# Log-sum-exp of 16384 rows: other groups of rows for each exponential and row sum

## The chip, the cores and the metric

The kernel runs on one core of a Trainium2 chip. The metric is the device time of one execution in microseconds, taken as the median of several runs. Besides that there is one profiled execution with its trace. The engines that matter here are ScalarE (ACT in the profile), VectorE (DVE), TensorE (PE), SyncE (SP), which issues the transfers, and the 16 DMA engines, which carry them.

## The reference

x has the shape 32 x 512 x 1024 in float32, 67 MB in all. For each of the 16384 rows of 1024 elements the log of the sum of the exponentials is wanted:

```python
max_x = np.max(x, axis=-1, keepdims=True)
return (max_x.squeeze(-1) + np.log(np.sum(np.exp(x - max_x), axis=-1))).astype(np.float32)
```

## The kernel before

The kernel computes exponentials, row sums and logarithms without the maximum first. It then tests all sums for lying between 1e-15 and 1e15 and, only where one does not, goes over everything again with the maximum (the branch at line 258). With this data the branch is not taken.

The 16384 rows are spread over 128 partitions, so each partition has 128 rows; "a row" below is one row on each of the 128 partitions, that is 128 x 1024 elements or 512 KB. The rows come in by 18 transfers ("loads", counted from 0), whose sizes in rows are the first entries of the list LOADS (lines 17 to 22): 16, 16, 16, 16, 13.5, 12.5, 9, 7.5, 5.5 and so on down to 0.375. They go into a ring of 48 rows in SBUF. A load starts at the place behind the last one, and at the ring's beginning again when it would not fit. Loads 0 to 2 fill rows 0 to 47 of the ring; load 3 has rows 0 to 15, load 4 rows 16 to 29.5, load 5 up to 42, and load 6 begins at row 0 again.

All loads are issued by SP, in order, from one queue (line 126). Before each, SP waits until the last readers of the ring rows that it will overwrite are through (lines 122 to 125). The first load is moved to the very start of the program (lines 318 to 332). A load that SP is waiting to issue holds up all loads behind it.

The second entry of each load says how its rows are worked, group by group:

- "Rn": ScalarE takes the exponential of n rows in one instruction, in place (line 192; the last group of a load takes the exponential of what is left of the load too, even where this is a part of a row that the next load completes), and VectorE then sums the n rows in one instruction (line 196).
- "A": ScalarE takes the exponential of one row and sums it in the same instruction, with a short second instruction that reads the sum (line 181). VectorE has nothing to do.
- "Tn": ScalarE takes the exponential of n rows, and VectorE sums each row by adding its halves with an accumulated result (line 204).
- "Y" and "Z": the two pieces of the last row, with sums by ScalarE (line 170).

ScalarE waits for each load to land (line 164), VectorE for the exponential of its group (lines 195 and 201). Each engine goes through its instructions in the order of the list. There are two logarithms: one of the first 112 sums (line 219), which ScalarE takes behind load 10's exponential, and one of the last 15 and 1 (lines 230 and 232). The range test goes over VectorE (lines 133, 138, 242, 251) and TensorE (lines 143, 147, 248).

Of the kernel before, what the change touches and what calls it, by code (L numbers as in the profile page):

```python
# [14 lines left out]


LOADS = [
    (16, "R16"), (16, "R8 R8"), (16, "R8 R8"), (16, "R8 R8"), (13.5, "R7 R6"),
    (12.5, "R7 R6"), (9, "A A A A A A A A A"), (7.5, "R3 R2 R2"), (5.5, "R4 T2"),
    (4.625, "T4"), (3.3125, "T3"), (2.4375, "T3"), (1.8125, "T2"), (1.3125, "T1"), (0.9375, "T1"),  # L20
    (0.5625, "T1"), (0.625, "Y"), (0.375, "Z"),
]


# [338 lines left out]
```

## Time and profile before

| | |
|---|---|
| median of 3 runs | 162.42 us (162.29 to 162.43) |
| the profiled execution | 162.54 us, its span 161.2 us |
| busy: VectorE, ScalarE, TensorE | 120.4, 116.2, 2.1 us |
| row sums, line 196 | 15 instructions, 108.8 us |
| exponentials, line 192 | 23 instructions, 103.8 us |
| exponentials with sum, line 181 | 9 instructions, 9.4 us, and 1.7 us for reading the sums |
| row sums by halves, line 204 | 17 instructions, 10.7 us, and 1.4 us for reading the sums |
| HBM read | 67.11 MB, 417 GB/s over the span |

The span runs from the first to the last instruction in the profile, and the device time holds 1.34 us more. The busy times of different engines run side by side and cannot be added up. In the views below, a group's line gives its total busy time, the mean of one instruction in ns, and the idle time of its engine just ahead of it with what ended it.

### The profile page before, as it was taken

The numbers are of one execution on the slowest core, as the hardware profiler recorded it, in microseconds if no ns is written. First come the engines' busy times: TensorE is split into PE (matmuls) and PEld (weight loads), VectorE is DVE, ScalarE is ACT, GpSimd is POOL, SyncE is SP. The second block draws the span as 40 slices with busy tenths as digits, with TensorE's granted clock in tenths as the row PEclk, the third lists the DMA queues.
The fourth block names the chain that finished last, engine by engine and source line by source line (L and its number), as shares of the span: only waits on it lengthen the run. The fifth ranks groups of instructions, "written<-read, shape, count | busy, mean of one in ns | idle before, by whom it ended". The sixth has DMA issues, their size and how long they took to land.

```text
span 161.2 us, 227 instructions
## 1 busy us (share of the span) xinstructions
PE 2.1 (1%) x24; PEld 1.0 (1%) x24; DVE 120.4 (75%) x57; ACT 116.2 (72%) x49; POOL 0.2 (0%) x4
## 2 busy tenths in 40 slices
PE   0000000000000000000000000000000000000022
PEld 0000000000000000000000000000000000000011
DVE  0000000009999999999999999999999995999894
ACT  3000059990799709995199949983999999989995
POOL 0000000000000000000000000000000000000000
DMA  7996996996996996996999999997999999999991
GB/s 260 520 520 276 504 520 276 504 520 276 504 520 276 504 520 276 504 520 276 463 439 439 439 423 407 445 534 331 439 439 419 434 407 430 442 419 410 410 397 25
DMA packets 2883, 67.19 MB, mean 417 GB/s; under 512 B 577, under 2 KB 705, under 8 KB 1345
## 3 DMA queue, kind: packets, MB, share of 16 engines
q1 hardware_dynamic: 2880, 67.18, 97.3%
q14 instruction: 3, 0.02, 0.0%
HBM read 67.11 MB, written 0.07 MB: 417 GB/s over the span
## 4 chain that ended last, share of the span: by engine, by line
DVE 51%; DMA 29%; ACT 16%; issue 2%; PE 0%
DVE sumexp L196 51%; DMA ring<-in_x_dram 29%; ACT ring L192 15%; ACT last_exp L170 1%; ACT res L219 0%; PE count L147 0%; DVE fine L251 0%
## 5 line engine op out<-in xcount | busy, mean ns | idle before, releaser
L196 DVE TENSOR_REDUCE sumexp<-ring 128x8 f32<-128x8192 f32 (+6 forms) x15 | 108.8, 7326 | 36.3 <-ACT ring L192 36.3
L192 ACT ACTIVATE ring<-ring 128x8192 f32<-128x8192 f32 (+15 forms) x23 | 103.8, 4571 | 41.8 <-DMA ring<-in_x_dram 41.8
L204 DVE SCALAR_TENSOR_TENSOR ring<-ring 128x512 f32<-128x512 f32 x17 | 10.7, 689 | 0.6 <-ACT ring L192 0.6
L181 ACT ACTIVATE ring<-ring 128x1024 f32<-128x1024 f32 x9 | 9.4, 1041 | 0.0
L114 ACT ACT_TABLE_LOAD x1 | 1.3, 1283 | 1.5 <-PEq L57 1.5
L143 PE MATMUL count<-far,bad 128*1 128x1 f32 x2 | 0.2, 164 | 153.7 <-DVE clamped L138 153.7
L147 PE MATMUL count<-sumexp,ones 128*1 128x1 f32 x20 | 1.8, 164 | 3.5 <-DVE ring L204 3.4
L181 ACT ACTIVATION_READ_ACCUMULATOR ring<-ring 128x1 f32 x9 | 1.7, 186 | 0.0
L204 DVE DVE_READ_ACCUMULATOR ring<-ring 128x1 f32 x17 | 1.4, 83 | 0.0
L115 DVE MEMSET ones<- 128x1 f32 x1 | 0.1, 59 | 1.5 <-PEq L57 1.5
L170 ACT ACTIVATE last_exp<-ring 128x640 f32<-128x640 f32 (+1 forms) x2 | 1.2, 591 | 0.0
L143 PEld LDWEIGHTS count<-far,bad 128*1 128x1 f32 x2 | 0.1, 80 | 153.7 <-DVE clamped L138 153.7
L147 PEld LDWEIGHTS count<-sumexp,ones 128*1 128x1 f32 x20 | 0.8, 81 | 4.4 <-DVE ring L204 4.2
L251 DVE TENSOR_SCALAR fine<-count 1x1 int32<-1x1 f32 x1 | 0.1, 147 | 0.6 <-PE count L147 0.6
L170 ACT ACTIVATION_READ_ACCUMULATOR last_exp<-ring 128x1 f32 x2 | 0.4, 186 | 0.0
L138 DVE SCALAR_TENSOR_TENSOR clamped<-clamped,sumexp 128x119 f32<-128x119 f32 x1 | 0.3, 284 | 0.0
L232 ACT ACTIVATE res<-sumexp 128x1 f32<-128x1 f32 x1 | 0.3, 294 | 0.0
L219 ACT ACTIVATE res<-sumexp 128x112 f32<-128x112 f32 x1 | 0.3, 279 | 0.0
L242 DVE SCALAR_TENSOR_TENSOR clamped<-sumexp 128x9 f32<-128x9 f32 x1 | 0.2, 169 | 0.1
L133 DVE TENSOR_SCALAR clamped<-sumexp 128x119 f32<-128x119 f32 x1 | 0.2, 222 | 0.0
L230 ACT ACTIVATE res<-sumexp 128x15 f32<-128x15 f32 x1 | 0.2, 198 | 0.0
L248 PE MATMUL count<-far,bad 128*1 128x1 f32 x2 | 0.2, 164 | 0.0
(8 smaller groups left out, 0.7 us busy)
## 6 DMA issues: line engine op xcount, KB each, us to landing
ring<-in_x_dram SPq DMA_DIRECT2D x1, 6912.0 KB, 26.0
ring<-in_x_dram SPq DMA_DIRECT2D x1, 6400.0 KB, 23.9
ring<-in_x_dram SPq DMA_DIRECT2D x1, 4608.0 KB, 17.7
ring<-in_x_dram SPq DMA_DIRECT2D x1, 3840.0 KB, 19.3
ring<-in_x_dram SPq DMA_DIRECT2D x1, 2816.0 KB, 25.6
ring<-in_x_dram SPq DMA_DIRECT2D x1, 2368.0 KB, 25.2
ring<-in_x_dram SPq DMA_DIRECT2D x1, 1696.0 KB, 21.7
ring<-in_x_dram SPq DMA_DIRECT2D x1, 1248.0 KB, 24.4
```

The lines of the kernel that those rows point to most:

```text
L114: nc.scalar.preload_act_table_set("natural_log_exp_and_others")
L133: dve.did(nc.vector.tensor_scalar(out=clamped[:, 0:LATE], in0=sumexp[:, 0:LATE], scalar1=LOW, scalar2=HIGH, op0=ALU.max, op1=ALU.min,))
L138: dve.did(nc.vector.scalar_tensor_tensor(out=clamped[:, 0:LATE], in0=clamped[:, 0:LATE], scalar=0.0, in1=sumexp[:, 0:LATE], op0=ALU.bypass ...
L143: pe.did(nc.tensor.matmul(count, lhsT=bad[:, 0:1], rhs=far, start=True, stop=False))
L147: return pe.did(nc.tensor.matmul(count, lhsT=ones, rhs=sumexp[:, c : c + 1], **kw))
L170: at = act.did(nc.scalar.activation(out=last_exp[:, here - p : end - p], in_=ring[:, here:end], func=AF.Exp, accum_out=sumexp[:, LAST : NC ...
L181: at = act.did(nc.scalar.activation(out=v, in_=v, func=AF.Exp, accum_out=sumexp[:, c : c + 1]))
L192: at = act.did(nc.scalar.activation(out=v, in_=v, func=AF.Exp))
L196: who = (dve, dve.did(nc.vector.reduce_sum(out=sumexp[:, c : c + s], in_=rows, axis=AX.X)))
L204: who = (dve, dve.did(nc.vector.scalar_tensor_tensor(out=lo, in0=lo, scalar=1.0, in1=rows[:, r, H:d], op0=ALU.mult, op1=ALU.add, accum_out ...
L219: ln_early = act.did(nc.scalar.activation(out=res[:, 0:W], in_=sumexp[:, 0:W], func=AF.Ln))
L232: ln_last = act.did(nc.scalar.activation(out=res[:, LAST:NC], in_=sumexp[:, NC : NC + 1], func=AF.Ln, bias=sumexp[:, LAST:NC]))
```

## The change

Only the list LOADS changes; the rest of the kernel is the same text. The sizes of the loads and their order stay as they are.

```diff
 LOADS = [
-    (16, "R16"), (16, "R8 R8"), (16, "R8 R8"), (16, "R8 R8"), (13.5, "R7 R6"),
-    (12.5, "R7 R6"), (9, "A A A A A A A A A"), (7.5, "R3 R2 R2"), (5.5, "R4 T2"),
-    (4.625, "T4"), (3.3125, "T3"), (2.4375, "T3"), (1.8125, "T2"), (1.3125, "T1"), (0.9375, "T1"),
-    (0.5625, "T1"), (0.625, "Y"), (0.375, "Z"),
+    (16, "R16"), (16, "R16"), (16, "R16"), (16, "R5 R11"), (13.5, "A A A R10"), (12.5, "R6 R7"),
+    (9, "A A A R6"), (7.5, "A A A A A A R1"), (5.5, "R2 R4"), (4.625, "T4"), (3.3125, "T3"),
+    (2.4375, "T3"), (1.8125, "T2"), (1.3125, "T1"), (0.9375, "T1"), (0.5625, "T1"), (0.625, "Y"),
+    (0.375, "Z"),
 ]
```

Loads 1 and 2 get one exponential and one row sum of 16 rows each in place of two of 8. Load 3 is cut into 5 and 11 rows in place of 8 and 8. ScalarE sums twelve rows in place of nine, and they lie in loads 4, 6 and 7 (three, three and six) in place of all in load 6. The other rows of loads 4 to 7 are summed by VectorE in groups of 10, 6 and 7, 6, and 1. Load 8 becomes groups of 2 and 4 rows, both summed by line 196, where before it had one such group of 4 and two rows summed by line 204. From load 9 on nothing changes. In all, line 196 has 12 instructions in place of 15, line 192 has 19 in place of 23, line 181 has 12 in place of 9 and line 204 has 15 in place of 17.

## The prediction

> **What bounds the kernel now.** I read the page first, then a stage table cut at the landings, then the timelines of ScalarE, VectorE and SP one by one, then the DMA packets. The chain of waits puts 51% on VectorE:
>
> ```profile
> span 161.2 us, 227 instructions
> DMA  7996996996996996996999999997999999999991
> DVE 51%; DMA 29%; ACT 16%; issue 2%; PE 0%
> ```
>
> That chain is one of several that run side by side. The stage table is what decides. Its columns are the stretch, its length, the busy time of PE, PEld, DVE, ACT, POOL, then the clock, the DMA share and GB/s; the cuts are the landings of successive loads (each read as issue plus time to landing):
>
> ```profile
> 22.07:41.40 19.33, 0.00 (x0) 0.00 (x0) 5.42 (x1) 13.86 (x1) 0.00 (x0) 1.00 1.00 434
> ...
> 80.11:96.45 16.34, 0.00 (x0) 0.00 (x0) 16.34 (x3) 13.95 (x2) 0.00 (x0) 1.00 0.99 429
> 96.45:111.58 15.13, 0.00 (x0) 0.00 (x0) 15.13 (x2) 11.81 (x2) 0.00 (x0) 1.00 0.97 418
> ...
> 131.61:138.31 6.70, 0.00 (x0) 0.00 (x0) 4.76 (x3) 6.70 (x5) 0.00 (x0) 1.00 0.98 421
> 138.31:143.96 5.65, 0.00 (x0) 0.00 (x0) 5.65 (x3) 5.24 (x3) 0.00 (x0) 1.00 0.97 414
> 143.96:158.24 14.28, 1.51 (x16) 0.68 (x16) 13.61 (x37) 14.26 (x9) 0.00 (x0) 1.00 0.95 387
> ```
>
> The DMA engines are full in every stretch from the first packet (about 1.0 us) to the last landing at 158.24. A row of x costs 1.21 us there (19.35/16, 15.13/12.5), and 128 x 1.21 = 154.9, plus a little for each small load. ScalarE starts the last load's exponential at 158.50, 0.26 after it lands, and some 2.7 us of tail follow to 161.2. So the end is the transfer stream plus a tail; VectorE, although busy without a break from 35.98 to 132.7, is late for nothing. The stream keeps its pace with VectorE idle (434 GB/s in the first row) or full, so other work doesn't slow it. Therefore two questions decide: does the queue ever run dry, and do ScalarE and VectorE still keep up in the last 14 us, where both are nearly full?
>
> The load that meets the first question is load 6 (nine rows; loads are counted from 0), which reuses rows 0 to 8 of the ring and waits for both row sums of load 3:
>
> ```profile
> 104.83 0.33 SPq L126 DMA_DIRECT2D ring<-in_x_dram  x1
> ```
>
> ```profile
> ring<-in_x_dram SPq DMA_DIRECT2D x1, 4608.0 KB, 17.7
> ```
>
> It is issued at 104.83 and lands 17.7 us later, of which only 10.9 (9 x 1.21) are its own transfer: it stood 5.5 us behind load 5, whose last packets end engine by engine from 110.36 to 111.12 in the packet records.
>
> **The change part by part.** It alters only the list of loads. Sizes, order and number of loads stay; so does the work after row 112, except for when it starts. Durations, from the groups by form:
>
> ```profile
> L196 DVE TENSOR_REDUCE sumexp<-ring 128x8 f32<-128x8192 f32 x6 | 51.6, 8675 | 0.0
> L192 ACT ACTIVATE ring<-ring 128x16384 f32<-128x16384 f32 x1 | 13.9, 13856 | 19.4 <-DMA ring<-in_x_dram 19.4
> L196 DVE TENSOR_REDUCE sumexp<-ring 128x16 f32<-128x16384 f32 x1 | 17.2, 17220 | 34.4 <-ACT ring L192 34.4
> L181 ACT ACTIVATE ring<-ring 128x1024 f32<-128x1024 f32 x9 | 9.4, 1041 | 0.0
> ```
>
> From these, a row sum of r rows takes 1.067 r + 0.15 us, or 1.067 r + 0.06 from start to start; an exponential takes 0.853 r + 0.2, or 0.853 r + 0.1 from start to start; a row with ScalarE's own sum ("A") takes 1.04 from start to start. Loads 1 to 8 go through this by hand, landings fixed:
>
> 1. Loads 1 and 2, whole. Load 1 lands at 41.40, its exponential ends at 55.28 (before, the first half ended at 48.45); VectorE, free at 53.12, waits 2.2 us, and sums from 55.31 to 72.53. Load 2: exponential to 74.64, another wait of 2.2, sum from 74.67 to 91.88 (before, both halves were through at 87.57). Two instructions fewer save 0.1 in all, inside ScalarE's 5.4 us of idle time per load. SP is held for as long: load 4 is issued at 72.6 (before 70.48) and load 5 at 91.95 (before 87.65). They are needed when loads 3 and 4 end, near 79 and 95, so both have over 3 us left. Cost so far: nothing on the stream, 4.3 us of VectorE's lead.
> 2. Load 3, R5 and R11. Exponentials end at 84.6 and 94.1, so VectorE doesn't wait: R5 from 91.8 to 97.2, R11 from 97.2 to 109.07. Load 6, which waits for R11, is issued at about 109.14 (the trace shows 0.03 to 0.09 from the end of a sum to the issue): 4.3 us later than before. **This is the change's one dangerous place.** The first engine is out of work at 110.36, the last at 111.12; the lead is 1.2 to 2.0 us, where the smallest before was 5.5. Nothing but the later loads stands behind it in SP's queue.
> 3. Load 4, A A A R10. Three rows leave VectorE (3 x 1.067 = 3.2) and cost ScalarE 3 x (1.04 - 0.853) = 0.6, hidden in its idle time ahead of load 5 (3.3). R10 runs 109.0 to 119.8, R6 and R7 of load 5 to 133.8. Before, VectorE was through load 5 at 132.73 and then waited 1.94; it is now 1.0 later, inside that wait.
> 4. Loads 6 to 8. ScalarE has the same nine A rows in them, but six sit in load 7. Load 6 is done on ScalarE at 130.9 instead of 131.9, so it waits 0.7 for load 7 (131.61), and cannot use the second that it saved. It then runs six A's, R1, R2 and R4 without a gap to 144.15. Before it was ready for load 9 at 143.55 and waited 0.43 for its landing at 143.96; now it starts 0.17 late. VectorE: R6 to 140.2, R1 to 141.3, R2 to 143.5, a wait, R4 (two rows of it were two short sums with line 204 before) from 144.28 to 148.69.
> 5. The rest is unchanged in kind. ScalarE was within 0.05 us of the landings of loads 10 to 14 and had 0.1 us to spare before load 16 (157.74); a start 0.17 late leaves about 0.1 at the end. VectorE is 0.16 late from load 10 on and ends its last sum at about 158.7; it is needed at 159.1 by line 230, so this costs nothing.
> 6. SP's later issues: load 7 at 109.5 (before 112.3), load 8 at 119.9 (112.7), load 9 at 120.3 (118.8), loads 10 to 12 as before, load 13 at 133.85 (127.6). Load 13 is wanted only after load 12 lands at 153.3, load 8 after load 7 at 131.6. No cost. POOL's queue holds nothing, and TensorE's small products keep their places.
>
> **The unknown cost** is what a late load 6 loses. The trace before has no load that came to an almost empty queue, so I bound it by the two issues that met an empty one. The last store (line 236) was issued at 159.45 and its packets start at 160.29, 0.84 later, on all engines within about 0.1. By that, load 6 is on every engine by 110.1, before the first runs out: 0. The very first load, issued at 0.0, starts packets at 1.03 to 1.66, and they take 2.5 to 3.4 us where later ones of that size take 2.42; in effect data flows 1.62 to 2.39 us after the issue. If every engine repeated its own delay, the gap would be 109.14 + 1.62 - 110.36 = 0.4 on each, and load 6 and all after it would land 0.4 later. Nothing excludes the start of the program as the reason for that. I take 0: store and load both show the descriptors there in 0.8 to 1.7 us, and a landing counts the slowest of the 16 engines, which is free only at 111.12, 2.0 us after the issue; the engines that run dry earlier can lose 0.1 to 0.7 and still not be the last. Below nothing there is no room, since the stream before has no gap to close.
>
> The first-load row shows a first packet 0.06 to 0.97 us longer than a steady one. The Trainium skill (HBM Reference, Latency) gives 0.2 us for an average access to HBM and 2 us under high load; at the high figure, as an estimate, data would flow at 109.14 + 0.84 + 2 = 112.0, a gap of 0.9 and a time of 163.4. The row speaks against so much.
>
> **Sum.** 0 + 0.1. The profiled execution took 162.54 (span 161.2 and 1.34 around it), so 162.65; the median of the runs is 0.12 lower, so I forecast **162.5** on the scale of 162.42. What a measurement can tell from no change is about 0.2%, or 0.32 us.
>
> **Rivals.**
>
> - *Load 6 comes too late* and the transfer queue runs dry once, between 110.4 and 111.5. For it: the lead falls from 5.5 to 1.2 us, and the first load needed 1.62 to 2.39. Against: the store's 0.84 and the slack of the slowest engine. It decides from a delay of about 2.0 us between issue and data on the slowest engine, or from an engine that loses more than its slack. Price 0.4 plus the 0.1: 162.9, slower. Chance 0.29.
> - *VectorE becomes the bound at the end.* For it: it loses 4.3 us of lead by load 3, and 13.6 of the last 14.3 us are busy. Against: A rows give 3.2 back in load 4, it still waits 0.8 for R4's exponential, and has 0.4 before line 230. It takes 1.2 us more than I reckon, for example sums 2% slower for 60 us, to show at all; at twice that it gives 1.2: 163.6. Chance 0.05.
> - *It gains.* The most that could go is ScalarE's 0.26 between the last landing and the last exponential: 162.2, still within 0.2%. More would need a faster stream, and that has no gap. Chance 0.03 for a gain over 0.2% by anything that I don't see.
>
> The forecast (0 to 0.25 us slower, or a partial gap that stays under 0.32) has 0.63, its own range being 162.4 to 162.7. So faster 0.03, same 0.63, slower 0.34. For 8 in 10 the range goes up over the dry queue at 162.9 to 163.1, and down to 162.3.
>
> **What would show it.** In the profile after: two waits of 2.2 us on VectorE before the sums of loads 1 and 2; the issue of load 6 near 109.1; ScalarE idle 0.7 before load 7's first A and not before load 9; the last exponential near 158.6. Load 6's packets decide: if the first ones start later than 110.4 and the landings from load 6 on (122.5, 131.6) are 0.3 or more late, the queue ran dry and I am wrong by that. If the landings stand and the end is late, then ScalarE's or VectorE's sums in steps 4 and 5 are wrong.

## The result and the profile after

The changed kernel takes 164.11 us (median of 6 runs, 163.74 to 164.40) against 162.42 before: a ratio of 1.0104, 95% interval 1.009 to 1.0119. It is slower by 1.7 us, where I forecast 162.5 and gave 163.1 as the upper end of the range for 8 in 10. The profiled execution took 164.33 us.

Two lines of the page of the kernel after, the size of the profile and the chain of waits by engine:

```profile
span 163.0 us, 221 instructions
DMA 39%; ACT 29%; DVE 26%; another core or an unknown queue 3%; issue 0%; PE 0%; SPq 0%; DVEq 0%
```

The chain now runs through transfers more than through VectorE, and SP's queue (SPq) appears in it. The stage table of the kernel after, cut at its own landings, with the same columns as before:

```profile
21.99:41.29 19.30, 0.00 (x0) 0.00 (x0) 5.39 (x1) 13.86 (x1) 0.00 (x0) 1.00 1.00 435
...
80.01:96.34 16.33, 0.00 (x0) 0.00 (x0) 16.33 (x2) 13.95 (x2) 0.00 (x0) 1.00 0.99 429
96.34:111.48 15.14, 0.00 (x0) 0.00 (x0) 15.14 (x3) 12.28 (x7) 0.00 (x0) 1.00 0.97 413
111.48:124.56 13.08, 0.00 (x0) 0.00 (x0) 13.08 (x2) 10.96 (x2) 0.00 (x0) 1.00 0.99 422
124.56:133.69 9.13, 0.00 (x0) 0.00 (x0) 9.13 (x3) 8.44 (x7) 0.00 (x0) 1.00 0.99 424
133.69:140.39 6.70, 0.00 (x0) 0.00 (x0) 6.45 (x1) 6.68 (x13) 0.00 (x0) 1.00 0.97 406
...
146.14:160.36 14.22, 1.51 (x16) 0.68 (x16) 13.85 (x33) 14.22 (x10) 0.00 (x0) 1.00 0.84 344
```

The two stretches of the kernel before that end with the landings of loads 6 and 7:

```profile
111.58:122.51 10.93, 0.00 (x0) 0.00 (x0) 10.93 (x3) 10.90 (x2) 0.00 (x0) 1.00 1.00 431
122.51:131.61 9.10, 0.00 (x0) 0.00 (x0) 9.10 (x2) 9.10 (x18) 0.00 (x0) 1.00 1.02 440
```

Read the lengths (second number) one by one. Every stretch has within 0.1 us the length that it had before, but one: the stretch that ends with the landing of load 6 takes 13.08 us in place of 10.93. The loss is 2.15 us in one place; load 7 behind it takes 9.13 (before 9.10), load 8 takes 6.70 as before. The DMA share of 0.99 hides it, for two reasons: 13 of 16 engines lose little and go on with load 7, and a landing waits for the slowest. The delay lasts to the end: of the 16 reports of a landing, the last two come 1.4 and 1.7 us after the one ahead of them for load 6, and still 1.4 and 1.5 us after it for load 17, the last. So the idle time of the other engines shows only in the last stretch, with a DMA share of 0.84 where the kernel before has 0.95.

The chain in order of time (start, length, what) shows what stands ahead of that load:

```profile
74.56 34.42 DVE sumexp L196 x3
108.98 0.02 issue
109.00 0.02 SPq L44
109.01 0.05 issue
109.06 0.33 SPq L126
109.39 0.04 issue
109.43 24.25 DMA ring<-in_x_dram
133.69 0.02 issue
133.71 6.35 ACT ring L181 x12
```

Three row sums of VectorE (load 2, and both of load 3) lead to SP's issue of load 6 at 109.06; load 7, issued at 109.43, lands behind it at 133.69 and ScalarE waits for that. In the packet records the 16 engines run out of load 5 between 110.44 and 111.06. Thirteen go on with load 6 without a hole. The other three start it at 110.99, 112.38 and 112.67, which is 1.9, 3.3 and 3.6 us after the issue. Fourteen of the 16 first packets also take longer than the steady 1.36 us, by up to 0.75.

From the first load's landing to the last one's the stream takes 138.37 us, before 136.17: 2.20 more. The execution is only 1.79 longer (164.33 against 162.54), since the first load landed 0.08 earlier here and the last store landed 1.42 us after its issue in place of 1.72.

In two of the experiments below the spread of the runs is the effect itself; there I give the median and range of all runs, since the ratios leave out those more than 1.5% above the fastest (they are the later issue of load 7 and the changed kernel again).

### The profile page after: what moved, and what is told of

The parts are those of the page before. It is cut to its first block, busy times and chain, and to the rows that moved or that the text cites. A ratio compares the mean times of both kernels' runs of the same rounds, so it can differ in the third digit from the quotient of the medians.

```text
span 163.0 us, 221 instructions
## 1 busy us (share of the span) xinstructions
PE 2.1 (1%) x24; PEld 1.0 (1%) x24; DVE 118.2 (72%) x50; ACT 116.3 (71%) x51; POOL 0.2 (0%) x4
## 4 chain that ended last, share of the span: by engine, by line
DMA 39%; ACT 29%; DVE 26%; another core or an unknown queue 3%; issue 0%; PE 0%; SPq 0%; DVEq 0%
DMA ring<-in_x_dram 39%; ACT ring L192 25%; DVE sumexp L196 21%; DVE ring L204 4%; ACT ring L181 4%; SPq L126 0%; DVE clamped L138 0%; DVE clamped L133 0%; PE count L248 0%; DVE clamped L242 0%; PE count L147 0%; DVE fine L251 0%; DVEq L44 0%; SPq L44 0%
## 5 line engine op out<-in xcount | busy, mean ns | idle before, releaser
L196 DVE TENSOR_REDUCE sumexp<-ring 128x16 f32<-128x16384 f32 (+8 forms) x12 | 107.9, 9037 | 41.2 <-ACT ring L192 41.2
L192 ACT ACTIVATE ring<-ring 128x16384 f32<-128x16384 f32 (+15 forms) x19 | 100.8, 5358 | 38.6 <-DMA ring<-in_x_dram 38.6
L181 ACT ACTIVATE ring<-ring 128x1024 f32<-128x1024 f32 x12 | 12.5, 1046 | 5.2 <-DMA ring<-in_x_dram 5.2
L204 DVE SCALAR_TENSOR_TENSOR ring<-ring 128x512 f32<-128x512 f32 x15 | 9.4, 688 | 0.1
L181 ACT ACTIVATION_READ_ACCUMULATOR ring<-ring 128x1 f32 x12 | 2.3, 188 | 0.0
```

The source lines that it names most:

```text
L181: at = act.did(nc.scalar.activation(out=v, in_=v, func=AF.Exp, accum_out=sumexp[:, c : c + 1]))
L192: at = act.did(nc.scalar.activation(out=v, in_=v, func=AF.Exp))
L196: who = (dve, dve.did(nc.vector.reduce_sum(out=sumexp[:, c : c + s], in_=rows, axis=AX.X)))
L204: who = (dve, dve.did(nc.vector.scalar_tensor_tensor(out=lo, in0=lo, scalar=1.0, in1=rows[:, r, H:d], op0=ALU.mult, op1=ALU.add, accum_out ...
```

## The experiments

The experiments ran on four chips, on which the kernel before had medians of 162.35 to 162.47 us; each ratio is to the kernel before on the same chip.

Theory: load 6 is issued too late, the transfer queue runs dry, and all that follows is late by the gap. Rival A: it is slow because load 7 is issued 0.4 us behind it. Rival B: the moved A rows or the larger groups make an engine late, whatever the transfers do. "Lead" below is the time from the issue of load 6 until the first engine runs out of load 5, in the profiled execution. "Descriptors", in the expectations, stands for what an issue hands to the DMA engines; the records show only the packets that follow.

### Is it the issue of load 6?

**Load 3 in 9 and 7 rows** (`(16, "R5 R11")` to `(16, "R9 R7")`, the only edit to the changed kernel):

> The changed kernel with load 3 cut into 9 and 7 rows in place of 5 and 11, all else kept. Load 6 overwrites rows 0 to 8 of the ring, so it then waits for the first sum alone and is issued near 101.6 us instead of 109.1; load 7 waits for the second, near 109.1. Theory (the transfer queue ran dry because load 6 was issued too late): load 6 lands near 122.4, and the time falls back from 164.1 to about 162.5. Rival A (load 7 issued 0.4 us behind load 6 slows load 6 down): about 162.5 too, since the two are no longer issued together. Rival B (the moved A rows or the larger groups make ScalarE or VectorE late in the tail, and the late landings come from elsewhere): stays near 164.1.

Measured: 162.07 us (161.99 to 162.24); ratio to before 0.998 (0.997 to 0.9989). SP's timeline in this kernel, with the issues of loads 6 and 7 merged, and then load 6's time to landing:

```profile
101.47 7.85 SPq L126 DMA_DIRECT2D ring<-in_x_dram  x2
```

```profile
ring<-in_x_dram SPq DMA_DIRECT2D x1, 4608.0 KB, 20.9
```

Load 6 goes out at 101.47 and lands at 122.4, 10.92 us behind load 5: no gap. Loads 1 and 2 are whole, the A rows are where the change put them, and VectorE ends load 3 at the same time as in the changed kernel. So rival B falls, and so does any direct cost of the two large waits. All of the slowdown hangs on which ring rows load 3's first sum sets free.

**Loads 1 and 2 in halves, the rest as changed** (`"R16"` to `"R8 R8"` for loads 1 and 2):

> The changed kernel with loads 1 and 2 cut into halves again, as before; load 3 and all behind it as changed. Load 6 is issued near 106.1, still 0.4 us ahead of load 7. Theory (late issue of load 6): lead 4.3 us, no gap, about 162.5. Rival A (load 7 issued right behind load 6): still together, stays near 164.1. Rival B (moved A rows, large groups of loads 3 and 4): stays near 164.1.

Measured: 162.02 us (161.87 to 162.37); ratio 0.9979 (0.9968 to 0.9991). Load 6 at 105.87, load 7 at 106.25, lead 4.5, no gap. Rival A falls: two loads issued together are harmless when they are early.

**Load 7 issued later** (`(13.5, "A A A R10")` to `(13.5, "R5 A A A R5")`):

> The changed kernel with load 4 in the order R5 A A A R5 in place of A A A R10. Load 6 is issued near 109.1 as in the changed kernel, but load 7 has to wait for the first R5 of load 4 and is issued near 114.5 instead of 0.4 us behind load 6. Theory (late issue of load 6): the lead is unchanged, so about 164.1 (163.7 to 164.5). Rival A (load 7 right behind it): falls to about 162.5. Rival B: little change from 164.1.

Measured: median 163.72, and runs from 161.97 to 165.94; four of ten at 162.0 to 162.1, the others 163.7 and above. Load 6 at 108.85, alone, lead 1.6. Six of ten runs lose although load 7 leaves 5.3 us behind load 6, as the theory has it; the four without a loss, and the spread, nobody expected. In the profiled execution (163.76) one engine alone was late: its first packet came 3.2 us after the issue, with a further hole of 0.74 behind it.

**The changed kernel again**, as a control:

> The changed kernel once more, unaltered, as the control for the next three on the same chip. Load 6 is issued near 109.1, some 1.3 us before the first DMA engine runs out of load 5. 163.7 to 164.4 as before; if the delay is a matter of chance, as in the kernel that spread from 162.0 to 165.9, wider.

Measured: median 164.03, 161.99 to 165.13; three of ten runs at 162.0 to 162.5. So the changed kernel itself has runs with little or no loss; among the first six there was none, whether by chance or for another reason. Lead 1.4; in the profiled execution (165.13) three engines had their first packet 3.0 to 3.5 us after the issue.

### How the loss hangs on the lead

**Load 3 whole** (`(16, "R5 R11")` to `(16, "R16")`): load 6 leaves after all engines are empty.

> The changed kernel with load 3 as one group of 16 rows. Its sum starts only after the whole exponential and ends near 111.2, so load 6 is issued near 111.3, when all 16 DMA engines have run out of work. Theory in the form that descriptors take up to 3.6 us from issue to the slowest engine as in the changed kernel: load 6 lands about 4.3 us late against before, and the time is about 166.4 (165.8 to 167). In the form that they reach idle engines as the first load of the program did (data flows at most 2.4 us after the issue): 2.6 us late, about 165.0. In the form that a queue that ran dry costs a fixed 2 us: about 164.2.

Measured: 163.99 us (163.82 to 164.12); ratio 1.0093 (1.0071 to 1.0115). The DMA engines from 110 to 114 us in 40 slices of 0.1 us, first in this kernel, then in the one with 9 and 7 rows:

```profile
DMA  0000000000000000000999000900080000000098
GB/s 0 0 0 0 0 0 0 0 0 0 0 0 0 0 0 0 0 0 0 3318 1106 737 0 0 0 369 0 0 0 369 0 0 0 0 0 0 0 0 737 369
```

```profile
DMA  0000989990900000090999809000000989998900
GB/s 0 0 0 0 737 369 1475 1475 1106 0 737 0 0 0 0 0 0 737 0 1475 1475 1106 369 0 737 0 0 0 0 0 0 737 369 1475 1106 1106 369 737 0 0
```

A packet counts where it starts. Without a gap, starts come at 110.4 to 111.1 and every 1.36 us from there. Here nothing starts before 111.9: issue at 110.94, first packets of 14 engines 0.96 to 1.17 us later, of the last two 1.6 and 2.0, and the early ones take 1.9 to 2.4 us in place of 1.36. So data flows at its steady pace as from 1.6 to 2.0 us after an issue to idle engines: that is the first load's row of the prediction again (1.62 to 2.39), and not the "3.6 us for the slowest" form, which falls here. The time that I had put beside the first load's form, 165.0, is 1.0 too high all the same: the issue came 0.36 us earlier than reckoned, the delay was 2.0 in place of 2.4, and without a gap the changed list takes about 162.1 and not 162.4. The fixed 2 us (164.2) is nearest here and falls only with the next kernel.

**Load 3 in 1 and 15 rows** (`(16, "R1 R15")`), lead 0.3:

> The changed kernel with load 3 cut into 1 and 15 rows: the sum of the 15 ends near 110.1, so load 6 is issued some 0.3 us before the first DMA engine runs dry. Theory (an engine that is still busy may get the descriptors of a new load as late as 3.6 us after the issue): as bad as the changed kernel or worse by the lost lead, median 164 to 165.5, spread over more than 1 us. Rival (a dry engine costs a fixed 2 us): 164.0, narrow. Rival (the delay after the issue is the same 1.0 to 2.0 us as where all engines were idle, plus a long first packet): 163.4, narrow.

Measured: 163.17 us, narrow (163.06 to 163.35); ratio 1.0054 (1.0039 to 1.0069). Issue at 110.10, first packets 0.95 to 1.87 us later: the third theory's delay, and its 163.4 is 0.2 too high. A loss of 1.1 us is no fixed 2. Being issued 1 us later than in the changed kernel makes it faster.

**Load 2 in 15 and 1 rows, in 14 and 2, and in halves**, with load 1 in halves in the first two and whole in the third: leads of 2.2, 3.0 and 3.7.

> The changed kernel with load 1 in halves and load 2 cut into 15 and 1 rows: load 6 is issued near 108.2, a lead of about 2.1 us on the first idle engine. Theory (descriptors reach single busy engines up to 3.6 us after the issue, and the gap is that minus the lead): between 162.1 and 163.5, spread from run to run. Rival (fixed cost whenever an engine runs dry): either 162.1 or 164.1, nothing between. Rival A (load 7 issued right behind load 6 is the cause, whatever the lead): 164.1.

> The same with load 2 cut into 14 and 2 rows: load 6 is issued near 107.3, a lead of about 3 us. Theory: gap of at most 0.6, so 162.0 to 162.6. Fixed cost: 162.1 in most runs. Rival A: 164.1.

> The changed kernel with load 2 alone in halves: load 6 is issued near 106.8, a lead of about 3.5 us. Theory: no gap, 162.0 to 162.2 in all runs. Fixed cost: the same. Rival A: 164.1.

Measured: 162.13 (162.02 to 162.59), 162.16 (161.99 to 162.39) and 162.10 (161.98 to 162.25). In the profiled execution of the first, which took 162.59, one engine of 16 got its first packet 2.9 us after the issue and load 6 took 11.42 us. In the other two it took 10.92, no gap. Loads 6 and 7 leave together in all three, so rival A falls again.

**Four leads between**, by a memset on VectorE ahead of load 3's second sum (line 196), of 240, 528 and 816 columns in the changed kernel and of 384 in the one with 15 and 1 rows:

```diff
             if how == "R":
+                if (i, k) == (3, 1):
+                    dve.did(nc.vector.memset(pad, 1.0))
                 dve.wait(act, at)
```

> The changed kernel with a memset of 240 columns on VectorE ahead of load 3's second sum, which puts off the issue of load 6 by some 0.3 us: lead 1.1 us on the first engine to run dry. Theory C (descriptors come 1.0 to 2.0 us after the issue; an engine that is already dry then starts with a long first packet, and an engine that runs dry just as they come can lose up to 2 us more): still within the overlap of 1.0 to 2.0 with the engines' 0.0 to 0.6 of spread, so spread, 162.3 to 165. Theory D (plain delay, no more than 2.0 us plus a long first packet, whatever the engine does): 162.6, narrow.

> The same with 528 columns, 0.6 us: lead about 0.8. Theory C: most engines are dry when the descriptors come, so the spread shrinks: 162.6 to 163.5, perhaps a run above. Theory D: 162.8, narrow. By the line through the two narrow kernels (lead 0.3: 1.1 late; lead -0.6: 2.0 late) it is 162.7.

> The same with 816 columns, 0.9 us: lead about 0.5. Theories C and D alike: 162.9 to 163.1, narrow. If it spreads as widely as the changed kernel, the overlap of arrival and running dry is not what makes the spread.

> The kernel with load 2 in 15 and 1 rows and a memset of 384 columns, 0.45 us, at the same place: lead about 1.8. Theory C: the slowest arrivals (2.0 us) still meet engines that run dry, in some runs: most at 162.1, some up to 164. Theory D: 162.1 in all.

Measured, with most of the others in order of lead; the last column is the slowest engine's first packet, counted from the issue, in the profiled execution:

| lead, us | median, us | all runs | slowest engine, us |
|---|---|---|---|
| -0.6 (load 3 whole) | 163.99 | 163.82 to 164.12 | 2.0 |
| 0.3 (1 and 15 rows) | 163.17 | 163.06 to 163.35 | 1.9 |
| 0.5 (816 columns) | 163.76 | 163.54 to 163.94 | 2.2 |
| 1.0 (528 columns) | 164.40 | 163.20 to 164.59 | 3.0 |
| 1.1 (240 columns) | 164.31 | 164.02 to 164.54 | 3.4 |
| 1.4 (the change) | 164.03 | 161.99 to 165.13 | 3.5 |
| 1.6 (load 7 later) | 163.72 | 161.97 to 165.94 | 3.2 |
| 1.9 (15 and 1, 384 columns) | 162.05 | 161.95 to 163.91 | never dry |
| 2.2 (15 and 1 rows) | 162.13 | 162.02 to 162.59 | 2.9 |
| 3.0 (14 and 2 rows) | 162.16 | 161.99 to 162.39 | never dry |
| 8.9 (9 and 7 rows) | 162.07 | 161.99 to 162.24 | never dry |

The loss doesn't fall evenly with the lead, so theory D falls: between 0.3 and 1.1 it grows from 1.1 to 2.2 us although load 6 leaves earlier. At 1.4 and 1.6, runs with little or no loss stand beside runs that lose 1.6 and more, at 1.9 two runs of ten lose 1.3 and 1.8, at 2.2 one loses 0.5, and from 3.0 up none loses. Load 5 says the same of 3 us: in the changed kernel it leaves 3.3 us before the first engine runs out of load 4, and no engine has a hole there. Theory C had the spread in the right place but not the level: it gave 162.6 to 163.5 at 0.8 and 162.9 to 163.1 at 0.5, both too low. What the records show is that a new load reaches all engines within 2.0 us of its issue where they are idle or soon will be (leads of -0.6 and 0.3), and that some engines get it only after 2.3 to 3.6 us where they or others are still moving the load before (leads of 1.0 to 2.2). With most of these leads it is one to three engines of 16; at 1.1 it is seven. Why just those are late was not found.

### The fast variants

With the gap gone the changed list is 0.3 us faster than before, where I had worked out 0.1 slower. In the profile before, the last store lands 1.72 us after its issue, and a transfer of instructions (queue q14) starts at 159.83, between the two; in all later profiles the store lands after 1.40 to 1.42. Two kernels add five instructions at the start of the one with 9 and 7 rows, where their engine has nothing else to do:

```diff
+    for i in range(5):
+        dve.did(nc.vector.memset(pad[:, i : i + 1], 1.0))
```

(the other: `act.did(nc.scalar.activation(out=pad[:, i : i + 1], in_=ones, func=AF.Exp))` in the same loop, behind a wait for VectorE's first memset)

> The kernel with load 3 in 9 and 7 rows, plus five one-element memsets on VectorE at the start, where it idles until 36 us; VectorE then has as many instructions as in the kernel before. Question: why is that kernel 0.3 us faster than before, when its transfers end no earlier? Theory (length of VectorE's instruction stream decides whether a block of instructions is fetched just as the last store is on its way): the final store lands 0.3 us later again and the time goes from 162.07 back to about 162.4. Rival (it is something else in the changed list): stays 162.07.

> The kernel with load 3 in 9 and 7 rows, plus five one-element exponentials on ScalarE at the start, where it idles until 22 us. If the length of any engine's instruction stream brings the fetch ahead of the last store, 162.4; if it is VectorE's alone, 162.07.

Measured: VectorE 162.16 (161.97 to 162.41), ScalarE 162.35 (162.31 to 162.49). VectorE's stream makes no difference that the intervals can tell. ScalarE's costs 0.2 to 0.3, but not by the store: that lands 1.41 after its issue here too. ScalarE's own timeline shows where. In the kernel with the five exponentials, then without them:

```profile
151.20 6.75 ACT L196 ACTIVATE ring<-ring 128x2496 f32<-128x2496 f32 x5
```

```profile
151.20 6.59 ACT L192 ACTIVATE ring<-ring 128x2496 f32<-128x2496 f32 x5
```

The same five exponentials start at the same time and take 0.16 longer, because the second of them starts at 153.52 in place of 153.37. It waits for load 12: of its 16 landing reports 15 come by 153.21, when it has wholly landed in the other kernel, and one at 153.50. In the packet records a transfer of instructions (queue q14) of 0.31 us starts at 152.20, with load 12 under way; without the five exponentials the first such transfer after the start comes at 161.01, when the last store has landed. So it is probably this transfer that holds up one engine's part of the load. It is one profile, and that the transfer caused the delay is not shown.

The kernel before has the same pattern at its last store: of the 16 landing reports 15 come by 160.87 and one at 161.18, with the transfer of instructions of 0.34 us that starts at 159.83. Its five exponentials take 6.60, so ScalarE isn't late there. The 0.39 us between the profiled executions (162.54 and 162.15) are nearly the store's 0.32 and 0.09 from a first load that landed later. That the store is what makes its other runs slower too isn't shown.

**Loads 6 to 8 as before, in the kernel with 9 and 7 rows** (`(9, "A A A A A A A A A"), (7.5, "R3 R2 R2"), (5.5, "R4 T2")`):

> The kernel with load 3 in 9 and 7 rows, and loads 6 to 8 as before (nine A rows in load 6, then R3 R2 R2 and R4 T2); loads 0 to 5 as changed, so VectorE has fewer rows than in either kernel. ScalarE then has no idle time ahead of load 7 and is ready for load 9 before it lands. By the working of the prediction this takes away 0.1 us: 161.95 to 162.0 against 162.07. If ScalarE's 0.17 us of delay at load 9 is covered anyway: 162.07.

Measured: 161.97 us (161.92 to 162.13); ratio to before 0.9974 (0.9965 to 0.9983). It is faster than the kernels before and after. ScalarE waits 0.43 us for load 9 again in its timeline, as before and as expected. Against the kernel with 9 and 7 rows (0.998, 0.997 to 0.9989) the intervals overlap, and the profiles don't show the 0.1 us either: the last exponential starts 0.25 us after the last landing here, and 0.24 in the one with 9 and 7 rows.

## Why the prediction was wrong

**What bounds the kernel**: right. The stream from first to last landing takes 136.15 to 136.27 us in each profile without a gap, whatever the groups, and the end follows it.

**Steps 1 to 3, when things happen**: right within 0.2 us. VectorE waits 2.08 and 2.14 us before the sums of loads 1 and 2 (2.2 said); loads 4, 5 and 6 are issued at 72.45, 91.81 and 109.06 (72.6, 91.95, 109.14). The profile before was enough for that, and for naming step 2 the one dangerous place.

**The unknown cost of a late load 6**: this is the step that failed. "I take 0", with 0.4 as the upper bound, is 2.15 us at the landings and 1.7 in the time. Both rows that I bounded it by were issues to engines with nothing to do (the first load and the last store). They give that case well: 1.1 us at a lead of 0.3 is near what the first load's row says (1.62 less 0.3). Even this row allowed more than 0.4, which sets the shortest of its delays against the first engine to run dry: the longest gives 109.14 + 2.39 - 110.36 = 1.2. But the change issues load 6 while the engines are ending load 5, and no row before showed that. The runs show up to 3.6 us for single engines there, beyond the 2.39 of the cold start, the longest delay in the rows. The slack of the slowest engine, 0.6 us, was of no use, since the late engines were others. Below nothing there was indeed no room.

**The rivals**: "load 6 comes too late" is what happens, with the right mechanism and place, the right sign of its condition (2.0 us of delay), and a price of 0.4 in place of 1.7; its chance of 0.29 was too low where the smallest lead fell from 5.5 to 1.2 us and no row of the trace had a price for that. The Trainium skill's figure for HBM under high load (HBM Reference, Latency, 2 us) had given 163.4 by an estimate, nearer than the 162.9 of the rows, though its gap of 0.9 is counted from the last engine to run dry and the 0.4 of the rows from the first; the runs show a late first packet, not that HBM access is its cause. VectorE is not the bound: in the kernel with 9 and 7 rows it has the same work at the same times and nothing is lost.

**Steps 4 and 5**: right in kind. ScalarE waits 0.69 us for load 7 (0.7 said) and not for load 9. The 0.1 us that step 5 carries to the end, the only term of the sum above nothing, isn't there: in the kernel with 9 and 7 rows ScalarE starts load 9 at 144.05, 0.18 after its landing, but load 16 only 0.04 after it, and the last exponential 0.24 after the last landing, where before it was 0.26. **Step 6**: no cost, as said.

## What to carry to other kernels

In a kernel bound by its transfers, find for each load the time between its issue and the moment when the load before it runs out, and keep that well above the delay seen on idle engines: here that delay was up to 2 us, and it took 3 us of lead until no run lost anything. Large groups are free for the engines that work on them, but they set buffers free late and in one piece; cut the group so that its first part covers just the rows that the next load overwrites (9 and 7 in place of 5 and 11 gave all of the loss back). A price bounded by an idle resource is no bound for a busy one: then the range has to be left open to that side.

## What the runs showed of the hardware

- The loss from a late issue doesn't simply grow the later the issue is: 1.1 us at a lead of 0.3, 2.2 at 1.1, and between 0 and 3.9 at 1.6 (165.94 against 162.07). An issue 1 us later was 0.9 us faster (163.17 against 164.03).
- Where a load was issued 1.0 to 2.2 us before the engines ran out, one to three of the 16 DMA engines (seven at a lead of 1.1) got their part only 2.3 to 3.6 us after the issue in the profiles with a gap, and a landing waits for them; the mean DMA share in that stretch of the changed kernel still reads 0.99. The delay of the last two landing reports was still there at the last load (1.4 and 1.5 us).
- With five more instructions of ScalarE a transfer of instructions fell at 152.20, into the stream of loads, and one of 16 landing reports of the load under way came 0.29 us later (one profile); with five more of VectorE neither was so.
